# Hybrid decoder layer on one core: score products that alternate between row halves, low-rank products stacked over 128 rows, one product for a chunk's right-hand side, dt projected in 16 columns

## The chip, the cores and the metric

The kernel runs on one core of one Trainium2 chip. A core has five engines with queues of their own, each in order: TensorE (PE in the profile; its weight loads are PEld), VectorE (DVE), ScalarE (ACT), GpSimd (POOL), and SyncE (SP), which here issues the DMA transfers. Matmuls write to PSUM, everything else lies in SBUF or in DRAM. The metric is the device time of one execution in microseconds; the time before is 2901.62 us, the median of three runs (2898.83 to 2908.35).

## What is computed

One layer of a hybrid decoder for a prompt of 2048 tokens and, with the same weights, eight sampled tokens. One input projection feeds two head groups, RWKV-7 time mixing and a Mamba-2 scan; their outputs go through one output projection, a LayerNorm, a squared-ReLU MLP and a second LayerNorm. Cut to the parts that the change touches:

```python
proj = x @ w_in                                   # 1024 -> 3336 columns
u = pr + (prev - pr) * mu_shift                   # token shift
r, k, v, uw, ua, ug = split(u)                    # uw and ua: 64 columns each
w_log = -softplus(-(w0 + tanh(uw) @ w_up)) - 0.5  # w_up, a_up: 64 x 512
a = sigmoid(a0 + ua @ a_up)
# per token and head (8 heads of 64), state S is 64 x 64:
Sa = S @ (-kk)
S = S * decay + Sa * (kk * a) + v * k
y = S @ r
dt = softplus(dt + dt_bias)                       # 8 columns of proj
```

The other parts of the layer are the same before and after.

## The kernel before, in words

The prompt goes in four blocks of 512 tokens. First `project` runs over the four blocks: 27 tiles of output columns, each 8 contraction tiles long. The fp32 operands are split into a high and a low fp32r part (`split`, lines 189 and 190: one ACT copy and one subtraction on DVE or POOL), and a product is three one-pass matmuls (`mm3`, lines 156 to 158). The tile of dt has 8 columns; it is projected in the same way, so its 24 matmuls a block have 8 output columns and 512 moving ones. `evict` takes each tile from PSUM. For every pair of heads `pair` makes decay and `a`: two fp32 products with 64 contraction rows, `waup[0:64]` with the upper half of the tile `uwa` and `waup[64:128]` with the lower half (lines 526 and 527). An fp32 product leaves two records in the profile. `pair` writes its results to DRAM (`s_ar`, `s_bk`, `s_v` and others), chunk by chunk.

The mixers then work on chunks of 64 tokens, eight a block, 32 in all. `rwkv` loads a chunk (`ar`, `bk`, `uv`) and makes the score products, line 591: eight fp32 products, four pairs of heads by two row halves, with 64 contraction rows each. Half j writes the PSUM tile `pss[j]`. Both are of tag "m", which has two buffers, shared with the other mixers. Masked, the scores go to `sc`; a triangular inverse follows (`masked`, tiles xs), and ends in `xf`. `chain` carries the state `S` (tag "st") through the chunks: the right-hand side `pr` is the sum of two products per head, scores times v and `ar` times S (lines 675 and 677); `rr`, `pu`, the new `uv`, the outputs `py` and the new state follow. `mamba` and `rwkv_post` are the other mixers.

`tail` is the output projection and the MLP of a block. The mixers of the next block are woven into the bulk matmuls of `project` and `tail` by `drive`, which gives each a step for so many microseconds of bulk. The order within an engine's queue is then set by a list scheduler when the program is built: it places whatever its estimate says is ready. Two products that stand side by side in the source can thus stand apart in PE's queue.

Of the kernel before, what the change touches and what calls it, by code (L numbers as in the profile page):

```python
# [18 lines left out]
FIRST = 4  # L19
POOLA, POOLO, POOLF = 4, 2, 0  # L20
# [87 lines left out]
class K:  # L108
# [41 lines left out]
    def mm(self, out, l, r, start=True, stop=True):  # L150
        self.nc.tensor.matmul(out, l, r, start=start, stop=stop)  # L151
# [71 lines left out]
    def setup_mix(self):  # L223
# [51 lines left out]
        self.waup = c("waup", (128, 512))  # L275
        nc.sync.dma_start(self.waup, A["waup"])
# [49 lines left out]
    def wpieces(self, j, halves=(0, 1)):  # L326
        out = []
        w = TILES[j][1]
        for h in halves:
            if w == 128:  # L330
                src = self.A["w_in"][j if j < T_DT else j - 1, :, h * 512:(h + 1) * 512]
            else:
                src = self.A["w_dt"][:, h * 32:(h + 1) * 32]
            out.append(self.wpiece(src, (4, w)))
        return out

    def project(self, b, ahead):
# [13 lines left out]
        for j in range(NT):  # L351
            w = TILES[j][1]
            if b == 0 and j < len(self.first):
                pieces = self.first[j]
            else:
                pieces = self.wpieces(j)
            if j == NT - 2:
                nxt = ahead()
            banks = []
            for o, n, _ in segs:  # L360
                ps = self.ps("b")
                for k in range(KT):
                    l = [pieces[k // 4][i][:, k % 4, :] for i in range(2)]
                    r = [act[k][:, i, o:o + n] for i in range(2)]
                    self.mm3(ps[:w, :n], l, r, k == 0, k == KT - 1)
# [14 lines left out]
    def evict(self, b, j, mains):  # L380
        nc, st = self.nc, self.blkst[b]
        if j < T_DT:
# [22 lines left out]
            if j == T_UWA:  # L405
                nc.scalar.activation(u[0:64], u[0:64], AF.Tanh)
            elif j == T_UG:
# [11 lines left out]
        else:  # L419
            i = j - T_Z  # L420
            th = self.pair_tile()[0][:, :TB]
            for o, m, ps in mains:
# [4 lines left out]
                              th.rearrange("p (u t) -> p u t", u=4))  # L427

# [36 lines left out]
    def delta(self, b, mains):  # L465
        nc, st = self.nc, self.blkst[b]
        raw = self.pair_tile()[0]
        for o, m, ps in mains:
            nc.scalar.activation(raw[0:8, o:o + m], ps, AF.Copy)
        pt = self.ps("a", (128, 4, 8))  # L470
        for u in range(4):
            self.tr(pt[:, u, :], raw[0:8, u * 128:(u + 1) * 128])
        dt = self.sm("dt", [128, 4, 8], bufs=4)
        nc.vector.tensor_tensor(out=dt, in0=pt, in1=self.dtb.unsqueeze(1).to_broadcast([128, 4, 8]), op=ALU.add)
# [28 lines left out]
    def pair(self, b, hp):  # L503
# [22 lines left out]
        self.mm(pw, self.waup[0:64, cs], uwa[0:64])  # L526
        self.mm(pa, self.waup[64:128, cs], uwa[64:128])
# [15 lines left out]
        for u in range(4):  # L543
# [22 lines left out]
        nc.sync.dma_start(self.s_bk[b][:, 64:128, hp, :].rearrange("c p x -> p c x"),  # L566
                          BK[64:128].rearrange("p c a t -> p c (a t)"))
        for a in range(2):
            nc.sync.dma_start(self.s_bk[b][:, 0:64, hp, (1 - a) * 64:(1 - a) * 64 + 64].rearrange("c p x -> p c x"),
                              BK[0:64, :, a, :])  # L570
# [3 lines left out]
    def rwkv(self, b, c):  # L574
# [8 lines left out]
        for j in range(2):  # L583
            nc.sync.dma_start(uv[H[j], j], self.s_v[b][c // 2, 64 * (c % 2):64 * (c % 2) + 64, :, 64 * j:64 * j + 64])
# [4 lines left out]
        for hp in range(4):  # L589
            for j in range(2):  # L590
                self.mm(pss[j][:, hp, :], bk[H[j], hp, :], ar[H[j], hp].rearrange("p a t -> p (a t)"))
        for j in range(2):
            nc.vector.tensor_tensor(out=sc[:, j], in0=pss[j],
                                    in1=self.con("scm").unsqueeze(1).to_broadcast([128, 4, 128]), op=ALU.mult)
            for g in range(4):
                p0 = 64 * (1 - j) + 16 * g
                nc.sync.dma_start(d_l[1 - j, g].rearrange("h s t -> s h t"), sc[p0:p0 + 16, j, :, 16 * g:16 * g + 16])
# [31 lines left out]
        def masked(x, m):  # L629
            p = pt()  # L630
            for hp, e in idx:
                self.mm(p[H[e], hp, :], sc[H[e], 1 - e, hp, 0:64], x[H[e], hp, :])
# [21 lines left out]
        g2 = masked(x2, "m2")  # L654
        yield
# [8 lines left out]
    def chain(self, b, c):  # L664
# [20 lines left out]
        nc.scalar.activation(uv[H[1], 0], pu[H[1]], AF.Copy)  # L685
        nc.vector.tensor_copy(uv[H[0], 1], pu[H[0]])
# [201 lines left out]
    def sample(self):  # L888
# [35 lines left out]
        for hp in range(4):  # L924
            self.mm(pw[:, hp, :], self.waup[0:64, hp * 128:(hp + 1) * 128], us[0:64, 0, :])
# [7 lines left out]
        for hp in range(4):  # L933
            self.mm(pa[:, hp, :], self.waup[64:128, hp * 128:(hp + 1) * 128], us[64:128, 0, :])
# [137 lines left out]
        nc.vector.tensor_scalar(out=dd[0:8, 0, :], in0=P[0:8, T_DT, :], scalar1=hb[0:8, 0:1], scalar2=None, op0=AD)  # L1072
# [505 lines left out]
```

## Time and profile before

| what | before |
|---|---|
| median of 3 runs | 2901.62 us |
| the profiled execution | 2905.99 us, of which the span is 2904.2 us |
| mean granted TensorE clock | 0.985 |
| first and last 400 us: PE busy | 388.54 of the first 400.00, 400.05 of the last 424.00 |
| DMA | 395.34 MB, mean 136 GB/s |

The span goes from the first to the last instruction. A row of the grouped view has the line, the engine, the operation, the tile written and those read, the shape (contraction rows * output columns, then output rows x moving columns), the count, the busy time in us and the mean of one in ns, and the engine's idle time before them. A row of the timeline has the start in us, the duration in us, and the same names; rows that follow on each other are merged, with their count.

### The profile page before, as it was taken

To read this page: it belongs to the slowest core of one execution; us is meant where nothing else is said; L and a number is where in the kernel's file an instruction comes from. 1 tells how busy PE (TensorE), PEld (TensorE's weight loads), DVE (VectorE), ACT (ScalarE), POOL (GpSimd) and SP (SyncE) were. 2 spreads that over 40 slices of the span, in tenths; PEclk is the share of its full clock that TensorE was granted. 3 is DMA by queue.
4 is the path that set the end of the run, shared out by engine and by line. 5 is a ranking of instruction groups with operands and counts; after the bars stand their busy time and mean duration, and the time that the engine had idled before them with its cause. 6 is when DMAs were issued, how large, how long until landed. Compare 5 with 4: busy or idle time off the path is not lost.

```text
span 2904.2 us, 53242 instructions
## 1 busy us (share of the span) xinstructions
PE 2825.7 (97%) x19648; PEld 2331.7 (80%) x19648; DVE 1963.2 (68%) x4765; ACT 1249.2 (43%) x2391; POOL 356.6 (12%) x510
## 2 busy tenths in 40 slices
PE   9999999999999999999999999998999999899997
PEld 6798987777788777788888888887877878888886
DVE  6767868867857777686866666568766655754446
ACT  4454544543536333344544344335443334543332
POOL 2221212211221000001300000022000000300001
PEclk9999999999999999999999999999999999999999
DMA  6654654554645444355523344254343334433232
GB/s 191 182 174 122 176 179 139 165 175 136 178 144 162 129 124 119 114 160 176 175 89 106 116 122 120 76 174 165 114 137 110 108 106 162 164 99 94 91 100 71
DMA packets 334169, 395.34 MB, mean 136 GB/s; under 512 B 85518, under 2 KB 191588, under 8 KB 333900
## 3 DMA queue, kind: packets, MB, share of 16 engines
q1 hardware_dynamic: 333908, 391.94, 44.8%
q8 instruction: 154, 2.52, 0.4%
q14 instruction: 107, 0.88, 0.1%
HBM read 331.06 MB, written 60.81 MB: 135 GB/s over the span
## 4 chain that ended last, share of the span: by engine, by line
PE 83%; DVE 9%; DMA 4%; issue 2%; ACT 2%; SPq 0%; POOL 0%; DVEq 0%; ACTq 0%; POOLq 0%
PE psb L156 19%; PE psb L157 18%; PE psb L158 18%; PE psm L151 7%; PE psa L156 4%; PE psa L157 4%; PE psa L158 4%; PE psc L151 2%; PE psa L151 2%; PE psm L163 1%; PE psy L694 1%; PE psb L151 1%; DVE w L190 1%; DMA wr<-in_w_in_dram 1%; DVE g L1176 1%
## 5 line engine op out<-in xcount | busy, mean ns | idle before, releaser
L189 ACT ACTIVATE w<-wr 128x512 fp32r<-128x512 f32 (+1 forms) x840 | 521.0, 625 | 693.2 <-PE psb L158 272.3
L190 DVE TENSOR_TENSOR w<-wr,w 128x512 fp32r<-128x512 f32 x714 | 511.0, 722 | 255.7 <-ACT w L189 247.0
L156 PE MATMUL psb<-act,w 128*128 128x512 f32 (+3 forms) x1796 | 637.4, 356 | 5.7 <-ACT act L189 5.0
L157 PE MATMUL psb<-act,w 128*128 128x512 f32 (+3 forms) x1796 | 630.0, 351 | 0.0
L158 PE MATMUL psb<-act,w 128*128 128x512 f32 (+3 forms) x1796 | 628.3, 350 | 0.0
L156 PEld LDWEIGHTS psb<-act,w 128*128 128x128 f32 (+1 forms) x1796 | 337.9, 189 | 61.5 <-ACT act L189 6.3
L158 PEld LDWEIGHTS psb<-act,w 128*128 128x128 f32 (+1 forms) x1796 | 338.4, 189 | 51.4 <-issue 3.3
L157 PEld LDWEIGHTS psb<-act,w 128*128 128x128 f32 (+1 forms) x1796 | 339.1, 189 | 46.1 <-DVE act L190 1.3
L156 PE MATMUL psb<-w,g 128*128 128x512 f32 x788 | 315.7, 403 | 0.2 <-ACT w L189 0.2
L157 PE MATMUL psb<-w,g 128*128 128x512 f32 x788 | 312.4, 396 | 0.0
L158 PE MATMUL psb<-w,g 128*128 128x512 f32 x788 | 311.4, 395 | 0.0
L190 POOL TENSOR_TENSOR w<-wr,w 128x512 fp32r<-128x512 f32 (+1 forms) x126 | 181.5, 1445 | 564.6 <-ACT w L189 546.4
L1453 DVE TENSOR_TENSOR g<-psb,g 128x512 f32<-128x512 f32 x173 | 118.9, 688 | 158.2 <-PE psb L158 157.8
L156 PEld LDWEIGHTS psb<-w,g 128*128 128x128 f32 x788 | 148.0, 188 | 36.5 <-ACT w L189 0.6
L158 PEld LDWEIGHTS psb<-w,g 128*128 128x128 f32 x788 | 148.0, 188 | 34.5 <-issue 0.3
L157 PEld LDWEIGHTS psb<-w,g 128*128 128x128 f32 x788 | 148.4, 188 | 32.5 <-issue 0.2
L190 DVE TENSOR_TENSOR g<-r,g 128x256 fp32r<-128x256 f32 (+1 forms) x172 | 97.2, 565 | 87.4 <-ACT g L189 86.3
L1403 ACT ACTIVATE r<-psb 128x512 f32<-128x512 f32 (+2 forms) x130 | 63.3, 488 | 208.9 <-PE psb L158 205.7
L156 PE MATMUL psa<-act,w 128*128 128x256 f32 (+2 forms) x336 | 115.7, 344 | 0.0
L157 PE MATMUL psa<-act,w 128*128 128x256 f32 (+2 forms) x336 | 114.1, 340 | 0.0
L158 PE MATMUL psa<-act,w 128*128 128x256 f32 (+2 forms) x336 | 113.5, 338 | 0.0
L156 PE MATMUL psb<-g,w 128*128 128x264 f32 (+3 forms) x324 | 108.9, 336 | 1.2 <-DVE g L400 0.8
(376 smaller groups left out, 5237.2 us busy)
## 6 DMA issues: line engine op xcount, KB each, us to landing
wr<-in_w_ff_dram SPq DMA_DIRECT2D x512, 256.0 KB
wr<-in_w_in_dram SPq DMA_DIRECT2D x208, 256.0 KB
wr<-in_w_out_dram SPq DMA_DIRECT2D x112, 256.0 KB
lr<-d_l SPq DMA_DIRECT2D x256, 64.0 KB
s_m<-g SPq DMA_DIRECT2D x48, 256.0 KB
ms<-s_m SPq DMA_DIRECT2D x16, 768.0 KB
wr<-in_xT_dram SPq DMA_DIRECT2D x32, 256.0 KB
s_ar<-g SPq DMA_DIRECT2D x16, 512.0 KB
```

The costliest lines, as they stand in the source:

```text
L151: self.nc.tensor.matmul(out, l, r, start=start, stop=stop)
L156: nc.tensor.matmul(out, l[0], r[0], start=first, stop=False)
L157: nc.tensor.matmul(out, l[0], r[1], start=False, stop=False)
L158: nc.tensor.matmul(out, l[1], r[0], start=False, stop=last)
L163: self.nc.tensor.transpose(out, in_, self.cst[p0:p0 + k, o + p0:o + p0 + k])
L189: nc.scalar.activation(hi, raw, AF.Copy)
L190: (eng or nc.vector).tensor_tensor(out=lo, in0=raw, in1=hi.bitcast(F32), op=ALU.subtract)
L694: acc = lambda o, l, r, start, stop: nc.tensor.matmul(o, l, r, start=start, stop=stop, skip_group_check=True)
L1176: eng.tensor_tensor(out=h, in0=h, in1=b[:p], op=ALU.add)
L1403: nc.scalar.activation(rl, ps, AF.Relu)
L1453: self.nc.vector.tensor_tensor(out=h, in0=ps, in1=h, op=ALU.add)
```

## The change

Four parts and what goes with them.

- Scores. `row` ties the eight score products together: each is queued right behind the one before it, with a high priority, in the order of the source, where the halves j = 0 and 1 alternate. A memset of one element of `pss[1]` on DVE stands ahead of the first, so the row is queued only when both PSUM tiles are to be had.
- Low-rank products. `w_up` and `a_up` are each laid over both halves of the 128 rows and split into high and low parts (`wup`). `stacked` lays the high part of the operand over one half of the rows and its low part over the other. A product is then two fp32r matmuls with 128 contraction rows in place of one fp32 product with 64. The sample takes the same parts, in fp32 and 64 rows, with two products in place of one.
- Right-hand side. In `sc` the 64 rows that held no scores for a half now take `ar`, by two ACT copies a chunk; in `uv` the rows that are later filled by `pu` first take S, by one copy on ACT and one on DVE. One product with 128 rows replaces two with 64. For this the halves of `bk`, `uv` and `sc` change places; the DMAs keep their sizes and number.
- dt. High and low parts of its weights are put side by side as 16 columns. Two matmuls per contraction tile replace three; the two halves are added on DVE. The weights come in one DMA and one split rather than two.

`dynamic_dma_scratch_size=256` sets aside less SBUF for transfers that POOL issues; the kernel has none.

```diff
+    def row(self, args, held):
+        prev = self.mm(*args[0])
+        self.tc.add_manual_dep(prev.ins, held.ins.name, mybir.DependencyInfo(
+            mybir.DependencyClass.NoSync, mybir.DependencyReason.DATA), reason="bank")
+        for a in args[1:]:
+            with self.tc.high_priority(RANK), self.tc.issue_after(prev.ins):
+                prev = self.mm(*a)
...
-        self.waup = c("waup", (128, 512))
-        nc.sync.dma_start(self.waup, A["waup"])
+        self.wup = []
+        for i in range(2):
+            raw = self.sb("wr", (128, 512))
+            for h in range(2):
+                nc.sync.dma_start(raw[64 * h:64 * h + 64], A["waup"][64 * i:64 * i + 64])
+            self.wup.append([self.mp.tile([128, 512], F32R, name=f"wup{i}{s}") for s in range(2)])
+            self.split(raw, *self.wup[i])
...
+                    if j == T_DT:
+                        l = pieces[:, k].rearrange("p s c -> p (s c)")
+                        self.mm(ps[:w, :n], l, r[0], k == 0, False)
+                        self.mm(ps[:w, :n], l, r[1], False, k == KT - 1)
+                    else:
+                        l = [pieces[k // 4][i][:, k % 4, :] for i in range(2)]
+                        self.mm3(ps[:w, :n], l, r, k == 0, k == KT - 1)
...
+    def stacked(self, u):
+        nc = self.nc
+        hl = self.sb("g4", (128, 2, 520), F32R)
+        W, a = hl[:, 0, :TB], hl[:, 1, :TB]
+        lo, hi = slice(0, 64), slice(64, 128)
+        for t, x, y in ((W, lo, hi), (a, hi, lo)):
+            nc.scalar.activation(t[x], u[x], AF.Copy)
+            nc.vector.tensor_tensor(out=t[y], in0=u[x], in1=t[x].bitcast(F32), op=ALU.subtract)
+        return W, a
...
-        self.mm(pw, self.waup[0:64, cs], uwa[0:64])
-        self.mm(pa, self.waup[64:128, cs], uwa[64:128])
+        for p, w, x in ((pw, self.wup[0], uwa[0]), (pa, self.wup[1], uwa[1])):
+            self.mm(p, w[0][:, cs], x, True, False)
+            self.mm(p, w[1][:, cs], x, False, True)
...
-        for hp in range(4):
-            for j in range(2):
-                self.mm(pss[j][:, hp, :], bk[H[j], hp, :], ar[H[j], hp].rearrange("p a t -> p (a t)"))
+        held = nc.vector.memset(pss[1][0:1, 0, 0:1], 0.0)
+        self.row([(pss[j][:, hp, :], bk[H[j], hp, :], ar[H[j], hp].rearrange("p a t -> p (a t)"))
+                  for hp in range(4) for j in range(2)], held)
...
         g2 = masked(x2, "m2")
+        for j in range(2):
+            nc.scalar.activation(sc[H[j], j, :, 0:64], ar[H[j], :, 0, :], AF.Copy)
...
+        nc.scalar.activation(uv[H[0], 0], S[H[0]], AF.Copy)
+        nc.vector.tensor_copy(uv[H[1], 1], S[H[1]])
         for hp in range(4):
             for j in range(2):
-                self.mm(pr[H[1 - j], hp, :], sc[H[j], j, hp, 0:64], uv[H[j], j, hp, :], True, False)
-            for j in range(2):
-                self.mm(pr[H[1 - j], hp, :], ar[H[j], hp, 0, :], S[H[j], hp, :], False, True)
+                self.mm(pr[H[j], hp, :], sc[:, j, hp, 0:64], uv[:, j, hp, :])
```

Three places of PE's queue show what the scheduler makes of it. The first is the score row of the fourth chunk of the first block, while the second block is projected (psm are the two score tiles, psb is the bulk tile that is being summed). Before, the four products of one half and the four of the other stand eight bulk matmuls apart:

```order
L151 MATMUL psm_4557<-ar_4537,bk_4539 128x128 x4
L158 MATMUL psb_4616<-g_248_1643,w_4588 128x256
L156 MATMUL psb_4616<-g_250_1650,w_4588 128x256
L157 MATMUL psb_4616<-g_250_1650,w_4588 128x256
L158 MATMUL psb_4616<-g_250_1650,w_4588 128x256
L156 MATMUL psb_4616<-g_252_1657,w_4588 128x256
L157 MATMUL psb_4616<-g_252_1657,w_4588 128x256
L158 MATMUL psb_4616<-g_252_1657,w_4588 128x256
L156 MATMUL psb_4616<-act_1732,w_4593 128x256
L151 MATMUL psm_4558<-ar_4537,bk_4539 128x128 x4
```

In the changed kernel the same row stands in one place, and the tiles of the two halves take turns:

```order
L166 MATMUL psb_4645<-act_1766,w_4597 128x264
L152 MATMUL psm_4560<-ar_4471,bk_4473 128x128
L152 MATMUL psm_4561<-ar_4471,bk_4473 128x128
L152 MATMUL psm_4560<-ar_4471,bk_4473 128x128
L152 MATMUL psm_4561<-ar_4471,bk_4473 128x128
```

Two more such pairs follow, and then the bulk tile goes on. Of the 32 rows, 7 alternated before; now all do.

The second place is a pair of heads in the first block, the products for decay (psa) and a (psb). Before, there is one fp32 product each, in two places among the bulk:

```order
L151 MATMUL psb_718<-g_32_310,waup 128x512
L156 MATMUL psb_746<-act_184,w_738 128x512
L157 MATMUL psb_746<-act_184,w_738 128x512
L163 MATMUL psa_708<-cst,arsy_84_652 8x128
L158 MATMUL psb_746<-act_184,w_738 128x512
L156 MATMUL psb_746<-act_189,w_738 128x512
L157 MATMUL psb_746<-act_189,w_738 128x512
L151 MATMUL psa_717<-g_32_310,waup 128x512
```

Now there are two fp32r matmuls in each place, of the shape of the bulk:

```order
L152 MATMUL psb_737<-g_35_328,wup_271 128x512
L152 MATMUL psb_737<-g_35_328,wup_272 128x512
L166 MATMUL psb_767<-act_184,w_759 128x512
L167 MATMUL psb_767<-act_184,w_759 128x512
L168 MATMUL psb_767<-act_184,w_759 128x512
L166 MATMUL psb_767<-act_189,w_759 128x512
L173 MATMUL psa_727<-cst,arsy_87_671 8x128
L167 MATMUL psb_767<-act_189,w_759 128x512
L168 MATMUL psb_767<-act_189,w_759 128x512
L166 MATMUL psb_767<-act_194,w_759 128x512
L152 MATMUL psa_736<-g_35_328,wup_264 128x512
L152 MATMUL psa_736<-g_35_328,wup_265 128x512
```

The third place is a right-hand side (psc) of the first block, which stands behind products of the triangular inverse (psm from xs). Before:

```order
L151 MATMUL psm_5317<-xs_5155,xs_5236 64x64 x8
L151 MATMUL psc_5328<-uv_4541,sc_4555 64x64 x2
L151 MATMUL psc_5328<-st_4925,ar_4537 64x64 x2
L151 MATMUL psc_5328<-uv_4541,sc_4555 64x64 x2
L151 MATMUL psc_5328<-st_4925,ar_4537 64x64 x2
```

The last four rows come once more, and transposes follow. Now eight products stand there:

```order
L173 MATMUL psa_5313<-cst,g_735_5120 128x128 x4
L152 MATMUL psm_5325<-xs_5158,xs_5241 64x64 x8
L152 MATMUL psc_5336<-uv_4475,sc_4558 64x64 x8
L173 MATMUL psm_5353<-cst,ms_5349 128x128 x4
L173 MATMUL psm_5365<-cst,ms_5349 128x128 x2
```

The products with S are gone; those that are left have 128 contraction rows, which differs from the 64 of the products ahead of them. Over the program, PE's right-hand sides stood in 13 groups of their own before, and otherwise in one group with products of 64 rows; they now stand in 41 groups of their own.

More of the change, by code (lines that the diff above doesn't have):

```diff
@@ L19 @@
 FIRST = 4
+RANK = 4000
 POOLA, POOLO, POOLF = 4, 2, 0
@@ L150, in mm @@
     def mm(self, out, l, r, start=True, stop=True):
-        self.nc.tensor.matmul(out, l, r, start=start, stop=stop)
+        return self.nc.tensor.matmul(out, l, r, start=start, stop=stop)
+    def row(self, args, held):
[5 more added lines that the diff above has]
+                prev = self.mm(*a)
     def mm3(self, out, l, r, first, last):
@@ L329, in wpieces, with wdt @@
         for h in halves:
[L330 to L333, printed above, removed]
+            src = self.A["w_in"][j if j < T_DT else j - 1, :, h * 512:(h + 1) * 512]
             out.append(self.wpiece(src, (4, w)))
         return out
+    def wdt(self):
+        raw = self.sb("wr", (128, 512))[:, :64]
+        self.nc.sync.dma_start(raw, self.A["w_dt"])
+        t = self.sb("w", (128, 2, 512), F32R)[:, 0, :128].rearrange("p (k s c) -> p s k c", k=KT, s=2)
+        self.split(raw.rearrange("p (k c) -> p k c", k=KT), t[:, 0], t[:, 1])
+        return t.rearrange("p s k c -> p k s c")
     def project(self, b, ahead):
@@ L351, in project @@
         for j in range(NT):
-            w = TILES[j][1]
-            if b == 0 and j < len(self.first):
+            w = 128 if j != T_DT else 16
+            if j == T_DT:
+                pieces = self.wdt()
+            elif b == 0 and j < len(self.first):
                 pieces = self.first[j]
@@ L362, in project @@
                 for k in range(KT):
-                    l = [pieces[k // 4][i][:, k % 4, :] for i in range(2)]
                     r = [act[k][:, i, o:o + n] for i in range(2)]
-                    self.mm3(ps[:w, :n], l, r, k == 0, k == KT - 1)
+                    if j == T_DT:
+                        l = pieces[:, k].rearrange("p s c -> p (s c)")
[4 more added lines that the diff above has]
+                        self.mm3(ps[:w, :n], l, r, k == 0, k == KT - 1)
                 banks.append(ps)
@@ L468, in delta @@
         for o, m, ps in mains:
-            nc.scalar.activation(raw[0:8, o:o + m], ps, AF.Copy)
-        pt = self.ps("a", (128, 4, 8))
+            nc.scalar.activation(raw[0:16, o:o + m], ps, AF.Copy)
+        pt = self.ps("a", (128, 4, 16))
         for u in range(4):
-            self.tr(pt[:, u, :], raw[0:8, u * 128:(u + 1) * 128])
+            self.tr(pt[:, u, :], raw[0:16, u * 128:(u + 1) * 128])
         dt = self.sm("dt", [128, 4, 8], bufs=4)
-        nc.vector.tensor_tensor(out=dt, in0=pt, in1=self.dtb.unsqueeze(1).to_broadcast([128, 4, 8]), op=ALU.add)
+        nc.vector.tensor_tensor(out=dt, in0=pt[:, :, 0:8], in1=self.dtb.unsqueeze(1).to_broadcast([128, 4, 8]), op=ALU.add)
+        nc.vector.tensor_tensor(out=dt, in0=pt[:, :, 8:16], in1=dt, op=ALU.add)
         self.softplus(dt.rearrange("p a b -> p (a b)"), 32)
@@ L924, in sample @@
         for hp in range(4):
-            self.mm(pw[:, hp, :], self.waup[0:64, hp * 128:(hp + 1) * 128], us[0:64, 0, :])
+            for i in range(2):
+                self.mm(pw[:, hp, :], self.wup[0][i][0:64, hp * 128:(hp + 1) * 128].bitcast(F32), us[0:64, 0, :], i == 0, i == 1)
         w = V6[:, 1]
@@ L933, in sample @@
         for hp in range(4):
-            self.mm(pa[:, hp, :], self.waup[64:128, hp * 128:(hp + 1) * 128], us[64:128, 0, :])
+            for i in range(2):
+                self.mm(pa[:, hp, :], self.wup[1][i][64:128, hp * 128:(hp + 1) * 128].bitcast(F32), us[64:128, 0, :], i == 0, i == 1)
         a = t(4, 8)
@@ L1071, in sample @@
         dd = t(2, 8)
-        nc.vector.tensor_scalar(out=dd[0:8, 0, :], in0=P[0:8, T_DT, :], scalar1=hb[0:8, 0:1], scalar2=None, op0=AD)
+        pd = self.ps("m", (128, 8))
+        self.mm(pd[0:8], self.con("s16", 0, 16), P[0:16, T_DT, :])
+        nc.vector.tensor_scalar(out=dd[0:8, 0, :], in0=pd[0:8], scalar1=hb[0:8, 0:1], scalar2=None, op0=AD)
         self.softplus(dd[0:8, 0, :], 8, 8)
```

23 lines of the change are left out of this document (12 added, 11 removed).

## The prediction

> **What bounds the kernel now.** I read the page first: the busy row, then the chain that ended last.
>
> ```profile
> span 2904.2 us, 53242 instructions
> PE 2825.7 (97%) x19648; PEld 2331.7 (80%) x19648; DVE 1963.2 (68%) x4765; ACT 1249.2 (43%) x2391; POOL 356.6 (12%) x510
> PE 83%; DVE 9%; DMA 4%; issue 2%; ACT 2%; SPq 0%; POOL 0%; DVEq 0%; ACTq 0%; POOLq 0%
> ```
>
> TensorE (PE) is busy for 97% of the span and carries 83% of the chain; 2904.2 - 2825.7 = 78.5 us is all that it is not busy. The longest causes in the waits view of PE (columns: who waited, for what; sum in us, times, longest) are these.
>
> ```profile
> PE psb L163 <- DVE g L1257: 7.9, 3, 4.7
> PE psm L151 <- DVE sc L593: 6.0, 5, 4.5
> PE psb L156 <- ACT act L189: 5.0, 1, 5.0
> ```
>
> None is a wait that returns every chunk. So time taken off PE's queue comes off the end, unless PE then meets new waits. "Busy" is not the price of a matmul, though: consecutive ones overlap. The price is the distance between two starts, which the timeline gives. Three prices follow, for work that the change removes.
>
> ```profile
> 1003.43 1.16 PE L151 MATMUL psm<-ar,bk 64*128 64x128 f32 x16 [0.66 <-DMA bk<-s_bk]
> 1004.52 0.50 PE L156 MATMUL psb<-act,w 128*128 128x512 f32 x1
> ...
> 907.95 1.74 PE L151 MATMUL psm<-ar,bk 64*128 64x128 f32 x16
> 909.62 0.39 PE L156 MATMUL psb<-act,w 128*128 128x256 f32 x1
> ...
> 387.69 0.28 PE L157 MATMUL psb<-g,w 128*128 128x256 f32 x1
> 387.90 1.16 PE L151 MATMUL psm<-ar,bk 64*128 64x128 f32 x8
> 388.98 0.38 PE L158 MATMUL psb<-g,w 128*128 128x256 f32 x1
> 389.21 0.28 PE L156 MATMUL psb<-g,w 128*128 128x256 f32 x1
> 389.33 0.28 PE L157 MATMUL psb<-g,w 128*128 128x256 f32 x1
> ...
> 390.37 1.16 PE L151 MATMUL psm<-ar,bk 64*128 64x128 f32 x8 [0.17 <-DVE sc L593]
> 391.45 0.38 PE L157 MATMUL psb<-act,w 128*128 128x256 f32 x1
> ```
>
> These are the score products of three chunks (an fp32 product leaves two records, so eight products are 16). In the chunk at 1003 the row halves alternate: 1004.52 - 1003.43 = 1.09 us. At 907 three of one half come in a row, three of the other, then one and one: 1.67 us. At 387 and 390 each half has its four in a place of its own: 1.08 us twice. Two halves that alternate run side by side; four of one half do not. And a visit of narrow products costs something around itself: the step of a 256-column matmul is 0.12 us (389.21 to 389.33), but 0.21 just before the visit and 0.23 just after it, so 0.20 us outside the visit's own time.
>
> **Scores.** Followed through the whole trace, 7 chunks alternate, 14 take 1.67 us, 9 are split into two visits, and two are irregular (about 2.1 and 1.4 us without idle time). In the changed order all 32 alternate. 14 x 0.58 = 8.1; 9 x (2.16 + 0.20 - 1.09) = 11.4; the two others 1.3: 20.8 us. The grouped row says the same by another way:
>
> ```profile
> L151 PE MATMUL psm<-ar,bk 64*128 64x128 f32 x512 | 58.0, 287 | 5.9 <-DVE xs L634 2.5 <-DMA bk<-s_bk 2.0 <-DVE sc L593 1.3
> L151 PE MATMUL psb<-g,waup 64*128 64x512 f32 x32 | 18.0, 641 | 0.0
> L151 PE MATMUL psa<-g,waup 64*128 64x512 f32 x32 | 18.0, 641 | 0.0
> L151 PE MATMUL psm<-ms,waup 64*128 64x8 f32 x16 | 2.1, 255 | 0.0
> L157 PE MATMUL psb<-act,w 128*8 128x512 f32 x20 | 7.9, 396 | 0.0
> L685 ACT ACTIVATE uv<-psc 64x256 f32<-64x256 f32 x32 | 12.1, 379 | 41.7 <-PE psc L151 41.3
> L686 DVE COPY uv<-psc 64x256 f32<-64x256 f32 x32 | 13.1, 410 | 1.2 <-ACT uv L685 1.2
> ```
>
> 58.0 us busy against 32 x 1.16 = 37.1 is 20.9. I take **21 us**, from 19 to 23.
>
> **Low-rank products.** The two waup rows are 32 products of 512 columns, two records each.
>
> ```profile
> 64.34 1.12 PE L151 MATMUL psb<-g,waup 64*128 64x512 f32 x2
> 65.39 0.50 PE L156 MATMUL psb<-act,w 128*128 128x512 f32 x1
> 65.73 0.40 PE L157 MATMUL psb<-act,w 128*128 128x512 f32 x1
> ...
> 66.55 0.39 PE L157 MATMUL psb<-act,w 128*128 128x512 f32 x1
> 66.86 1.12 PE L151 MATMUL psa<-g,waup 64*128 64x512 f32 x2
> ...
> 68.25 0.39 PE L156 MATMUL psb<-act,w 128*128 128x512 f32 x1
> 68.48 0.40 PE L157 MATMUL psb<-act,w 128*128 128x512 f32 x1
> ```
>
> A product alone holds PE for 65.39 - 64.34 = 1.05 us; 24 do so, and four pairs that stand together take 1.50 us a pair: 31.2 us. After it there are 64 one-pass (fp32r) products of 128 rows and 512 columns, of the shape of the bulk, whose step is 68.48 - 68.25 = 0.23 us: 14.9. The 28 visits also go: 0.08 before (66.55 to 66.86 is 0.31) and 0.11 after (0.34) is 5.3 us, of which I leave out a quarter for those that stand beside other narrow products. 31.2 - 14.9 + 4 = **20 us**, from 16 (visits worth nothing) to 22. The operand must be split once a block: two ACT copies and two DVE subtractions of 64x512, eight each in all, well under 1 us apiece; ACT at 43% and DVE at 68% hide them. Uncovered, they would cost about 2 us a block. The start gains 256 KB of loads and two splits; PE waits for nothing there after its first 5.0 us, so I take 0, at most 2.
>
> **dt.** 24 products a block become 16, each still of 512 columns and so 0.23 us (8 output columns take the 396 ns of the row above, as the bulk's 128 do): 8 x 4 x 0.234 = **7.5 us**.
>
> **Right-hand side.** Sixteen products a chunk become eight.
>
> ```profile
> 592.39 0.40 PE L158 MATMUL psb<-act,w 128*128 128x512 f32 x1
> 592.72 0.51 PE L151 MATMUL psm<-xs,xs 64*64 64x64 f32 x10
> ...
> 593.29 0.28 PE L151 MATMUL psc<-uv,sc 64*64 64x64 f32 x4
> 593.41 0.28 PE L151 MATMUL psc<-st,ar 64*64 64x64 f32 x4
> ...
> 593.88 0.28 PE L151 MATMUL psc<-st,ar 64*64 64x64 f32 x4
> 594.09 0.77 PE L163 MATMUL psm<-cst,ms 128*128 128x128 f32 x5
> ```
>
> Four records take 0.12 us (593.29 to 593.41), the last four 0.21 with the way out. Sixteen records fewer are 0.47 us a chunk, 15 us in all. But here the products share their visit with xs products of the same 64x64 shape, as in some 23 of the 32 chunks. The new ones are 128x64, a shape of their own, in 41 groups where before 13 stood alone: 28 visits more, at 0.20 us outside and some 0.05 for the entry, is 7 us back. I take **8 us**, from 0 to 15.
>
> [...]
>
> **Sample and the rest.** The sample's eight waup products (2.1 us) become sixteen: 2 us more. Per chunk ACT gets three copies of 64x256 and DVE one, 0.38 and 0.41 us by rows L685 and L686, and DVE a memset of one element: 36 us of ACT and about 15 of DVE over 2300 us, under other work. What is not hidden is their place. The copies of ar into sc wait on ACT for the last masked product, and splits of weights queue behind them; the copies of S into uv lie between the state update and the right-hand side that PE takes next in order. Bulk stands between in most chunks. I put 0.1 us a chunk on this, **3 us more**, from 5 less (places of the present waits shift) to 18 more (half a microsecond a chunk).
>
> **The sum.** 21 + 20 + 7.5 + 8 - 2 - 3 = 51.5 us off the profiled execution's own 2905.99 us (the span and 1.8 us around it): 2854.5. That execution is 4.4 us above the median of the runs shown, 2901.62, so 2850.
>
> **Rivals.** *Waits take half.* PE is fed by splits on ACT and DVE; work that leaves PE leaves them less time. For it: DVE at 68% is in places the next engine. Against: no repeated PE wait for a split in the list above. Half of 54.5 us (the sum without its last term): 2874. *The shapes cost nothing.* If the new groups mostly lie beside other narrow ones, the right-hand side gives its 15 us, and with a few waits less the time is 2835. *PE is not what sets the end*, and the work leaves as idle time: 2900; 97% busy speaks against it. *Slower.* A row of scores now begins only when both psm banks are free, by the memset in DVE's queue, and PE takes its queue in order: a row that is late holds all the bulk behind it. It decides at 54.5 / 32 = 1.7 us a chunk; at 3 us a chunk the time is 2901.6 - 54.5 + 96 = 2943. The longest wait of PE for DVE's score product is 4.5 us, but all five together are 6.0, and the changed order puts the rows into running bulk groups. *The change doesn't do what it says* is ruled out by the order: all rows alternate, and the shapes are there.
>
> **How the numbers follow.** Forecast (2840 to 2865) 0.58; cheaper shapes 0.17; half lost 0.15; no effect 0.05; slower 0.05. Within 0.3% is about what a measurement here can tell from no change: faster 0.90, same 0.05, slower 0.05. The ends: all terms at their best with 5 us fewer waits are 23 + 22 + 7.5 + 15 - 2 + 5 = 70.5, so 2831; all at their worst with 18 us of waits are 19 + 16 + 7.5 + 0 - 2 - 18 = 22.5, so 2879. What lies outside is under 2 in 10.
>
> **What would show it.** psm<-ar,bk falls from 58.0 us busy to about 37, with all 32 visits at 1.09 us. The waup rows give way to 64 records of 128x512 near 400 ns; dt rows read 128*16, 48 rather than 72 at full width. psc<-st,ar is gone, and psc<-uv,sc is 128*64 at about 24 us. PE's busy time falls by about 50 us while what it is not busy stays near 78. Wrong would be PE waits on uv, sc or the memset that repeat every chunk, or score rows that alternate and still take more than 1.2 us.

## The result, and the profile after

The changed kernel takes 2881.95 us (median of four runs, 2878.82 to 2886.13); beside it the kernel before took 2904.98 us (four runs, 2898.83 to 2909.46). The ratio is 0.9923, with a 95% interval of 0.9906 to 0.994: faster, by 23 us. The forecast was 2850, its range 2831 to 2879; the time lies 3 us above the range, as much as the median of the kernel before moved between its first three runs (2901.62) and these four.

The page of the changed kernel, with the busy row and the shares of the chain:

```profile
span 2880.1 us, 52319 instructions
...
PE 2786.3 (97%) x19114; PEld 2310.9 (80%) x19114; DVE 1979.4 (69%) x4841; ACT 1285.9 (45%) x2493; POOL 364.5 (13%) x508
...
PE 79%; DVE 10%; DMA 4%; issue 4%; ACT 2%; SPq 1%; POOL 0%; DVEq 0%; POOLq 0%; ACTq 0%
```

PE is busy 39.4 us less (2825.7 before), but what it is not busy rose from 78.5 to 2880.1 - 2786.3 = 93.8 us. PE's waits (who waited, for what; sum, times, longest):

```profile
PE psb L166 <- ACT w L199: 13.9, 5, 9.3
PE psb L173 <- DVE g L1308: 9.9, 4, 4.7
PE psb L166 <- ACT act L199: 5.5, 2, 5.2
...
PE psb L167 <- DVE w L200: 4.4, 1, 4.4
...
PE psm L152 <- issue: 2.7, 3, 1.3
```

Before, the rows that answer to the first and the fourth are these.

```profile
PE psb L156 <- ACT w L189: 2.7, 2, 2.5
PE psb L157 <- DVE w L190: 2.3, 1, 2.3
```

New are one wait of 9.3 us for a split of weights, in the first row, and the one of 4.4. All of PE's waits for splits on ACT, DVE and POOL (those over 0.15 us, without the first of the program) make 8.4 us before and 22.7 after. The groups that answer to those of before (busy, mean ns | idle ahead):

```profile
L152 PE MATMUL psm<-ar,bk 64*128 64x128 f32 x512 | 39.3, 294 | 8.7 <-DVE xs L677 4.1 <-issue 2.7 <-DVE psm L632 1.7
L152 PE MATMUL psc<-uv,sc 128*64 128x64 f32 x512 | 26.5, 233 | 1.6 <-ACT sc L700 1.4
L152 PE MATMUL psb<-g,wup 128*128 128x512 f32 x32 | 14.5, 535 | 0.0
L152 PE MATMUL psa<-g,wup 128*128 128x512 f32 x32 | 10.8, 420 | 0.0
L152 PE MATMUL psb<-act,w 128*16 128x512 f32 x40 | 9.8, 395 | 0.0
L152 PE MATMUL psm<-ms,wup 64*128 64x8 f32 x32 | 3.9, 254 | 0.0
```

Scores fell from 58.0 to 39.3 us, the waup rows gave way to 64 records of 128x512, dt has 16 columns, and psc<-st,ar is gone. The change does what it says.

To set all this against the forecast's terms I go through PE's records and give each the time from its start to the start of the next one, less the idle time ahead of that one, and less half of the time at half clock, that is, in which the trace has a granted clock of 0.50. "Work" is the sum of these; idle and half clock stand apart. The half is an estimate: in the changed kernel ten steps between the starts of the bulk's 128x512 matmuls take 2.33 us at full clock (1167.25 to 1169.58) and five take 2.14 at half (1177.13 to 1179.27), by which 0.46 of that time would be lost. From the two traces, in us:

| part | before | after | forecast | measured |
|---|---|---|---|---|
| scores | 55.2 | 35.1 | -21 | -20.1 |
| low-rank, with its neighbours and the sample's | 53.5 | 38.7 | -20 + 2 | -14.8 |
| dt | 22.7 | 15.1 | -7.5 | -7.6 |
| right-hand side, and the xs products beside it | 108.7 | 103.4 | -8 | -5.3 |
| bulk | 2261.5 | 2262.4 | 0 | +0.9 |
| the rest | 292.4 | 294.0 | 0 | +1.6 |
| **work** | 2794.0 | 2748.7 | **-54.5** | **-45.3** |
| idle between records | 58.8 | 73.8 | +3 with the next | +15.0 |
| lost to half clock | 31.4 | 37.2 | | +5.8 |

The work that left is 9 us short of the forecast. The waits were put at 3 us and are 21. So the question of the experiments: do these 21 us belong to one part?

### The profile page after: what moved, and what is told of

It reads as the page before. It is cut to its first block, busy times and chain, and to the rows that moved or that the text cites. A ratio compares the mean times of both kernels' runs of the same rounds, so it can differ in the third digit from the quotient of the medians.

```text
span 2880.1 us, 52319 instructions
## 1 busy us (share of the span) xinstructions
PE 2786.3 (97%) x19114; PEld 2310.9 (80%) x19114; DVE 1979.4 (69%) x4841; ACT 1285.9 (45%) x2493; POOL 364.5 (13%) x508
## 4 chain that ended last, share of the span: by engine, by line
PE 79%; DVE 10%; DMA 4%; issue 4%; ACT 2%; SPq 1%; POOL 0%; DVEq 0%; POOLq 0%; ACTq 0%
PE psb L166 18%; PE psb L167 18%; PE psb L168 17%; PE psm L152 7%; PE psa L166 4%; PE psa L168 4%; PE psa L167 4%; PE psc L152 2%; PE psa L152 2%; PE psb L152 1%; DVE w L200 1%; PE psm L173 1%; PE psy L741 1%; DVE lr L655 1%; DVE rX L656 1%
## 5 line engine op out<-in xcount | busy, mean ns | idle before, releaser
L166 PE MATMUL psb<-act,w 128*128 128x512 f32 (+2 forms) x1768 | 628.4, 356 | 6.3 <-ACT act L199 5.5
L167 PE MATMUL psb<-act,w 128*128 128x512 f32 (+2 forms) x1768 | 621.1, 352 | 0.6 <-DVE act L200 0.6
L168 PE MATMUL psb<-act,w 128*128 128x512 f32 (+2 forms) x1768 | 616.9, 349 | 0.0
L166 PEld LDWEIGHTS psb<-act,w 128*128 128x128 f32 x1768 | 335.9, 190 | 55.5 <-ACT act L199 6.0
L168 PEld LDWEIGHTS psb<-act,w 128*128 128x128 f32 x1768 | 336.3, 190 | 45.6 <-DVE w L200 0.2
L167 PEld LDWEIGHTS psb<-act,w 128*128 128x128 f32 x1768 | 337.0, 191 | 44.7 <-DVE act L200 2.6
L200 POOL TENSOR_TENSOR w<-wr,w 128x512 fp32r<-128x512 f32 x124 | 180.2, 1458 | 717.5 <-ACT w L199 703.6
L166 PEld LDWEIGHTS psb<-w,g 128*128 128x128 f32 x788 | 148.6, 189 | 46.1 <-ACT w L199 10.3
L655 DVE TENSOR_TENSOR lr<-rX,lr 128x4 f32<-128x4 f32 (+14 forms) x480 | 100.7, 210 | 10.8
```

The lines of the kernel that those rows point to most:

```text
L166: nc.tensor.matmul(out, l[0], r[0], start=first, stop=False)
L167: nc.tensor.matmul(out, l[0], r[1], start=False, stop=False)
L168: nc.tensor.matmul(out, l[1], r[0], start=False, stop=last)
L200: (eng or nc.vector).tensor_tensor(out=lo, in0=raw, in1=hi.bitcast(F32), op=ALU.subtract)
L655: nc.vector.tensor_tensor(out=row, in0=X[:, :, s + 1:16], in1=row, op=ALU.mult)
```

## The experiments

Each kernel is timed beside the kernel before, whose medians there lie between 2902.26 and 2904.98 us. Work, idle and half clock are those of its profiled execution; the clock is the mean over all its runs. For only low-rank the profiled execution, 2906.77 us, is 8 us above the median, so its half clock is not typical.

| kernel | median us | ratio, 95% interval | work | idle | half clock | mean clock |
|---|---|---|---|---|---|---|
| before | 2904.98 | | 2794.0 | 58.8 | 31.4 | 0.986 |
| **changed** | 2881.95 | 0.9906 to 0.9940 | 2748.7 | 73.8 | 37.2 | 0.982 |
| only scores | 2918.16 | 1.0030 to 1.0066 | 2777.5 | 80.4 | 36.8 | 0.982 |
| only low-rank | 2898.37 | 0.9966 to 0.9996 | 2778.6 | 62.1 | 43.8 | 0.984 |
| only dt | 2906.99 | 0.9990 to 1.0021 | 2786.2 | 58.7 | 36.6 | 0.984 |
| only right-hand side | 2903.08 | 0.9986 to 1.0012 | 2788.2 | 60.1 | 33.2 | 0.986 |
| only scores, no memset | 2911.51 | 1.0019 to 1.0047 | 2791.6 | 68.3 | 29.9 | 0.984 |
| changed, no memset | 2888.31 | 0.9938 to 0.9972 | 2758.0 | 69.1 | 38.9 | 0.982 |
| changed, weights first | 2885.10 | 0.9924 to 0.9955 | 2751.8 | 74.0 | 39.0 | 0.983 |
| changed less scores | 2891.95 | 0.9951 to 0.9974 | 2769.0 | 65.4 | 30.9 | 0.983 |
| changed less low-rank | 2890.92 | 0.9934 to 0.9968 | 2764.5 | 70.0 | 30.5 | 0.984 |
| changed less right-hand side | 2882.96 | 0.9902 to 0.9947 | 2755.1 | 70.8 | 38.6 | 0.983 |
| changed, rate 0.32 | 2888.76 | 0.9924 to 0.9959 | 2749.4 | 78.4 | 39.1 | 0.981 |
| changed, rate 0.40 | 2890.25 | 0.9936 to 0.9963 | 2749.1 | 72.2 | 44.8 | 0.980 |
| changed, rate 0.45 | 2892.32 | 0.9947 to 0.9973 | 2749.4 | 76.3 | 44.2 | 0.980 |
| changed, rate 0.55 | 2895.50 | 0.9959 to 0.9982 | 2749.9 | 78.5 | 44.6 | 0.981 |
| before, rate 0.45 | 2909.89 | 1.0015 to 1.0033 | 2796.3 | 62.5 | 31.9 | 0.985 |
| changed, later rate 0.20 | 2937.82 | 1.0093 to 1.0133 | 2746.8 | 118.4 | 45.9 | 0.971 |
| changed, second block untied | 2886.83 | 0.9926 to 0.9958 | 2751.4 | 64.7 | 48.4 | 0.981 |
| the same, rate 0.38 | 2889.33 | 0.9933 to 0.9968 | 2749.3 | 68.7 | 45.0 | 0.981 |

Among the kernels made from the changed one, those less scores and at rates 0.45, 0.55 and the later 0.20 have intervals that lie wholly above its own; for the others the intervals touch, and a difference of 1 to 9 us in their medians is an indication.

### Each part alone

The kernel before, with the lines of one part of the diff and no others. The first theory was that the waits come only with all parts together.

> The kernel before with the score rows alone changed (row and its memset). All three theories expect about 20 us less PE work in psm<-ar,bk (58 us busy to about 39). Theory A (work leaves as predicted; about 21 us came back only where all four parts together let the bulk run ahead of the mixers and the sample): PE idle within 5 us of before, time 15 to 20 us shorter. Rival B (the memset and the rows tied together hold the bulk up each chunk): time at most 10 us shorter, PE idle up by 8 us or more, with waits of psm on the memset. Rival C (the scheduler's static order decides where stalls fall, by chance): idle moves by more than 5 us in either direction at a few places, none of them at a score row.

> The kernel before with the low-rank products alone changed. Work removed as read from the two traces: about 15 us (not 20, since the visits around the products did not get cheaper), all of it while the input projection runs. Theory A: 12 to 15 us shorter, PE idle within 5 us of before. Rival B (splits of the operand and loads at the start cost time): under 8 us shorter, with PE waits on g or wup. Rival C: idle moves by more than 5 us at a few places away from the changed products.

> The kernel before with dt in 16 columns alone. Work removed: 7.6 us. Theory A: 6 to 8 us shorter. Rival B has no mechanism here and expects the same. Rival C: anything from 15 us shorter to 5 us longer, with idle time or half-clock time that moves by more than 5 us away from dt.

> The kernel before with the right-hand side alone as one product, with its copies of ar and S. Work removed by the traces: 11.5 us in the products, 6 us back in the xs products beside them, so 5 to 6 net. Theory A: 3 to 6 us shorter, idle within 5 us of before. Rival B (the copies lie in each chunk's chain and PE waits for them): no shorter or up to 10 us longer, with PE waits on sc or uv of 0.1 us a chunk or more. Rival C: idle moves by more than 5 us at places that have nothing to do with the copies. For the four single parts together: A expects a sum of 38 to 48 us, more than the 23 us of the whole change; B a sum near 23 us; C any sum.

Work fell by 16.5, 15.4, 7.8 and 5.8 us, 45.5 in all, against 45.3 for the whole: it adds up. The times don't: against the median beside them (2904.52) they are +13.6, -6.2, +2.5 and -1.4 us, 8.5 us *slower* in all (by the four intervals together some 0 to 18; dt and the right-hand side alone can't be told from no change), where the whole is 23 faster. The first theory fell. The scores alone gained 21.6 us of idle time. The group of score products, and the longest of their waits in the timeline (start, duration):

```profile
L152 PE MATMUL psm<-ar,bk 64*128 64x128 f32 x512 | 41.1, 299 | 20.3 <-issue 13.0 <-DVE xs L645 5.9 <-DVE g L1268 0.9
```

```profile
1132.87 0.06 DVE L600 MEMSET psm<- 1x1 f32 x1
...
1141.34 0.40 PE L166 MATMUL psa<-act,w 128*128 128x512 f32 x1
...
1147.24 0.69 DVE L749 TENSOR_TENSOR q<-q,q 128x512 f32<-128x512 f32 x1 [10.30 <-DMA q<-s_bv]
1147.85 0.69 DVE L200 TENSOR_TENSOR w<-wr,w 128x512 fp32r<-128x512 f32 x1
1148.46 0.68 DVE L756 TENSOR_TENSOR q<-psm,q 128x512 f32<-128x512 f32 x1
...
1149.24 2.08 PE L152 MATMUL psm<-ar,bk 64*128 64x128 f32 x16 [7.51 <-issue]
```

DVE waited 10.3 us for a transfer of another mixer, whose psm tile it reads only at 1148.46. The row starts 0.1 us after that read ends, so I take that tile for one of the two that the row needs; the row stood next in PE's queue, and the bulk behind it waited 7.5 us. The memset did not hold the row here: it ran at 1132.87, 16 us earlier, so the tile that it writes was had by then and the row stood for the other one. This is the forecast's rival "slower" (a late row holds the bulk behind it), with a price of 20.3 - 5.9 = 14.4 us in this order.

### The memset, the ring of weights, and the whole without the scores

No memset: the line `held = ...` and the dependency on it go, and the products stay tied. Weights first: four weight loads go ahead of the next block's inputs.

```diff
             if last:
+                for dh in range(1 if b == 0 else 0):
+                    w2s.append([self.wpiece(A["w_ff2"][f * 128:(f + 1) * 128, dh * 512:dh * 512 + 512], (1, 512))
+                                for f in range(4 * g, 4 * g + 4)])
                 nxt = before_last(b)
```

> The score rows alone, without the memset that holds a row back until both psm tiles are free (the products are still tied to each other). With the memset PE stood idle 20.3 us ahead of psm<-ar,bk (5.9 before). Theory D (a row that is queued in one piece waits for the second PSUM tile, which another mixer holds while DVE waits for a DMA; that wait holds all bulk behind it): if the memset is what puts the rows there, idle ahead of psm<-ar,bk falls under 9 us and the time to 2890 to 2902. If the tie itself does it, idle there stays over 14 us and the time within 5 us of 2918. Rival C (the stall at 1149 us is an accident of this order): idle ahead of the score rows falls, but as much comes back at other places, time 2908 to 2918.

> The changed kernel without that memset. In the changed kernel PE stood idle 8.7 us ahead of psm<-ar,bk. Theory D: the memset cost little in this order, so the time is 2875 to 2886 and idle there 4 to 9 us. Rival B (the memset is what slows the whole change): 10 us or more shorter, under 2872. Rival C: anything, 2865 to 2900, with idle time that moves at places away from the rows.

> The changed kernel, with the first four weight pieces of the last MLP group of the first block asked for before the output tiles of the next block (which wait for the sample and hold the ring wr). PE stood idle there for 9.3 us at 1313, with 17.1 us at half clock around it. Theory D (that stall is the ring's, and costs its 9.3 us and up to 8 us of half clock): the gap goes, time 2865 to 2873. Rival F (bulk has simply caught up with the sample's chain, and PE stands a little later for the same chain, at w_out or act of the next block): the gap moves behind 1313, time 2877 to 2886.

> The changed kernel with the score products in their old order (the other three parts kept). If the parts' times simply add, taking away a part that alone cost 14 us makes it faster: 2868 or less. If the scores' 20 us of PE work show once the other parts are there (theory D: work leaves, and stalls depend on what meets what): 2892 to 2903. Between these: the rows' waits take part of the 20 us.

Without the memset the group of the scores alone reads:

```profile
L152 PE MATMUL psm<-ar,bk 64*128 64x128 f32 x512 | 51.3, 295 | 11.1 <-DVE xs L642 6.6 <-DVE q L753 2.2 <-ACT m L984 1.4
```

Idle ahead of the rows fell by 9.2 us, but busy rose by 10.2: the rows no longer alternate throughout. So with the scores alone the memset costs 7 us, though it takes 14 us of work off, and in the whole it is worth 6, by medians whose intervals overlap. Without scores the whole is 10 us slower, so the part that alone cost 14 us is worth 10 in company. Weights first missed theory D and came out as rival F had it, at 2885 us: the wait of 9.3 us was gone, and one of 4.1 stood 2 us later.

That wait is the largest new one. In the changed kernel (ACT, DVE, SP, then PE):

```profile
1299.03 4.81 ACT L199 ACTIVATE act<-wr 128x512 fp32r<-128x512 f32 x7 [12.64 <-PE psb L168]
...
1302.08 0.75 DVE L1159 TENSOR_SCALAR m<-m,ms 128x1024 f32<-128x1024 f32 x1 [2.42 <-DMA m<-in_state_ssm_dram]
...
1306.99 4.29 DVE L200 TENSOR_TENSOR act<-wr,act 128x512 fp32r<-128x512 f32 x7
...
1308.88 0.90 SPq L206 DMA_DIRECT2D wr<-in_w_ff_dram  x2
...
1303.47 0.40 PE L168 MATMUL psb<-act,w 128*128 128x512 f32 x1
1313.19 1.22 PE L166 MATMUL psb<-w,g 128*128 128x512 f32 x2 [9.32 <-ACT w L199]
```

All seven buffers of `wr` hold inputs of the next block. ACT has copied them by 1304, but DVE, in order, is in the sample's state loop and subtracts only from 1306.99 on; until then SP cannot load the weights that PE needs. Before, the sample ended while bulk was still running (PE, DVE, PE):

```profile
1318.69 0.38 PE L163 MATMUL psm<-cst,m 8*128 8x8 f32 x4 [0.41 <-DMA m<-d_y]
...
1337.46 4.87 DVE L190 TENSOR_TENSOR act<-wr,act 128x512 fp32r<-128x512 f32 x7 [0.67 <-ACT act L189]
...
1342.51 0.99 PE L156 MATMUL psb<-w,g 128*128 128x512 f32 x3 [0.24 <-ACT w L189]
```

There 23.8 us lay between the sample's last transposes and the first product of the block's last weights, and PE waited 0.24 us. In the changed kernel PE is ready for that product at 1303.9, 39 us earlier than it started before; the sample's last transposes come at 1314.77, 4 us earlier. With the wait the granted clock went to half: 0.50 from 1306.10 to 1323.16. Windows of 17 us of the changed kernel (start:end, length, busy us of PE, PEld, DVE, ACT, POOL, then PEclk):

```profile
1289.00:1306.00 17.00, 14.87 (x64) 11.67 (x63) 13.33 (x17) 6.29 (x10) 0.00 (x0) 1.00 0.47 117
1306.00:1323.00 17.00, 9.81 (x34) 7.50 (x35) 11.71 (x27) 5.47 (x10) 0.00 (x0) 0.50 0.57 192
1323.00:1340.00 17.00, 16.96 (x111) 14.70 (x109) 9.28 (x20) 7.65 (x15) 5.21 (x4) 1.00 0.53 176
```

### The pace of the sample's chain

The next theory was that tied rows stretch the chain of the second block's mixers, behind which the sample stands. The order shows it: between the first and the last score row of that block 190 us of bulk matmuls stood in PE's queue before, and 221 stand there now, counted in the built order (in the traces 1060 and 1188 bulk matmuls). The rate at which the steps are woven in changes that and no work:

```diff
-RATE_M0, RATE_M, RATE_S = 0.2, 0.23, 0.35
+RATE_M0, RATE_M, RATE_S = 0.2, 0.23, 0.4
```

> The changed kernel with the step rate of the second block's mixers and the sample raised from 0.35 to 0.40 steps per us of bulk. In the built order, counted in us of bulk matmuls ahead, the eight score rows of the second block's mixers take 190 us before and 221 in the changed kernel (216 with the score rows alone changed, 190 to 195 with any of the other parts alone), and the sample's last transposes come 130 us of bulk ahead of the next block's MLP before, 110 after; at 0.40 it is 205 and 123. Theory G (tied score rows stretch the chain of the mixers and the sample, so that the bulk, now shorter, arrives at the end of the first tail before the sample is done): the idle time of PE between 1300 and 1320 (9.9 us) falls to under 5, time 2872 to 2879. Rival C (accidents of the order): that idle goes, but comes back elsewhere, time 2878 to 2890.

> The same at 0.45: the chain takes 192 us of bulk, the sample ends 142 ahead. Theory G: no stall at the end of the first tail, time 2868 to 2876. Rival C: 2878 to 2890. If a denser chain meets its own limits (transfers and DVE), waits at the score rows of the second block grow and the time is no better than at 0.40.

> The same at 0.55: the chain takes 180 us of bulk, the sample ends 150 ahead. Theory G: no more than at 0.45, 2866 to 2878, since the sample has then time to spare and the chain runs into its own transfers.

> The kernel before at 0.45, as a control: 167 us of bulk for the chain, the sample ends 167 ahead of the next MLP. Before, PE had only 0.7 us idle at the end of the first tail, so theory G expects no gain: 2900 to 2908. If the rate itself were worth something, 2895 or less.

The stall shrank as expected (idle between 1200 and 1400 us: 9.9 us in the changed kernel, then 7.6, 6.7 and 5.2), and the time got worse each time, by 8, 10 and 14 us. At the beginning of the same tail, between 800 and 1000 us, idle rose from 13.8 to 16.8, 20.7 and 24.8 us, and the half clock took 7 us more. The control lost 7 us as well. The gain was given back a few hundred us earlier.

### One part out of the whole, and other orders

> The changed kernel with the right-hand side in two products, as before (the other three parts kept). Theory H (each part takes its PE work off in every kernel; on top of it the time moves by some 8 us with the order, by idle time and half clock that no part owns): 5.6 us of work come back, so 2880 to 2895, with other work in PE's classes within 3 us of the changed kernel. Rival R (the copies and the new shapes of this part cause the idle time of the whole change): under 2879, with PE idle at least 8 us below the 73.8 us of the changed kernel.

> The changed kernel with the low-rank products as before. Theory H: 14.8 us of work come back, 2888 to 2904. Rival R2 (the parts stand in each other's way, so that the last one added is worth nothing): 2878 to 2886.

> The changed kernel with the step rate of the second block's mixers and the sample at 0.32 rather than 0.35; no product, copy or transfer is added or removed. Denser (0.40) cost 8 us. Theory H: the PE work is the same within 3 us, the time anywhere from 2874 to 2890, by idle and half clock alone. Theory G2 (the density of the mixers' steps in the first tail sets the stalls, and the lowest rate that still ends in time is best): 2870 to 2876, with less idle between 750 and 950 us and no more than before at 1313.

> The changed kernel with the step rate of the third and fourth block's mixers at 0.20 rather than 0.23, so that only the second and third tail are ordered otherwise. Theory H: PE work the same within 3 us, 2874 to 2890. Theory G2: 2870 to 2877, with less idle in the second and third tail (25.7 us there in the changed kernel).

No part owns the idle time: without the right-hand side it is 3 us lower, without the low-rank products 4, without scores 8. Low-rank is worth 9 us in company, the right-hand side 1. A rate of 0.32 costs 7 us with the work unchanged. The later rate of 0.20 missed every expectation, with the same work and 56 us more time. Of the 44.6 us of idle that it adds, 20 are the waits of the first row here; the second row is a score row that stood 9.3 us for a psm tile which DVE had still to read. PE's waits and the wait itself:

```profile
PE psb L166 <- ACT w L199: 34.1, 5, 21.2
PE psm L152 <- DVE q L792: 9.3, 1, 9.3
```

```profile
2470.57 0.80 PE L166 MATMUL psb<-w,g 128*128 128x512 f32 x1 [21.25 <-ACT w L199]
```

It is the wait of 1313 us again, at the end of the third tail. In SP's queue the block's last weights stand behind the inputs of the next block, and those behind the mixers that write them (SP's timeline of this kernel):

```profile
2460.11 4.72 SPq L322 DMA_DIRECT2D wr<-s_o  x8
2465.26 3.67 SPq L206 DMA_DIRECT2D wr<-in_w_ff_dram  x4
```

Mixers that are not through when the bulk comes to its last group hold it up.

### The second block untied

```diff
+        args = [(pss[j][:, hp, :], bk[H[j], hp, :], ar[H[j], hp].rearrange("p a t -> p (a t)"))
+                for hp in range(4) for j in range(2)]
+        if b == 1:
+            for x in args:
+                self.mm(*x)
+        else:
+            self.row(args, nc.vector.memset(pss[1][0:1, 0, 0:1], 0.0))
```

> The changed kernel, with the score rows of the second block alone (those in the first tail, ahead of the sample) in the old way: not tied and without the memset. By the built order their chain takes 195 us of bulk in place of 221 and the sample ends 130 us of bulk ahead of the next block's MLP in place of 110. About 4 us of score work come back there (8.7 to 12.8). Theory G (the tied rows stretch that chain, and the stall at the end of the first tail is its price: 9.3 us idle and about 5 us of half clock): idle from 1280 to 1350 us falls from 9.9 to under 6, PE's classes else unchanged, time 2870 to 2879. Theory H (any order has such stalls somewhere): 2880 to 2892, with the idle time back at other places.

> The same with the step rate there at 0.38 in place of 0.35: the chain takes 190 us of bulk and the sample ends 142 ahead. Theory G: the rest of that stall goes too, 2867 to 2877. Theory H, and what the rates 0.40 to 0.55 have shown: the stall shrinks, but denser steps cost as much at the beginning of the tail, 2880 to 2892.

Half of it held. In the first of the two the wait for the ring is gone, idle fell by 9.1 us to 64.7, and one wait is left there, for the sample's own transfer:

```profile
1293.87 0.41 PE L173 MATMUL psm<-cst,m 8*128 8x8 f32 x4 [3.81 <-DMA m<-d_y]
```

But the half clock rose by 11.2 us in that execution (over all its runs the mean clock is 0.981 against 0.982), 2.7 us of work came back, and the time is 5 us worse. At rate 0.38 that wait is there still, 4.9 us at 1280 us, and the time is 2889 us, in theory H's range. So in the changed kernel that stall comes with the tied rows (with the scores alone, the same rows leave only 3.5 us idle there), and its removal did not shorten the kernel.

No kernel tried here beats the changed one.

## Why the prediction was wrong, step by step

- **PE sets the end, so work that leaves comes off.** Right for the work: 45.3 us left, and it adds up part by part. Wrong in that a part's time follows from it: alone, the four parts together gained nothing.
- **Scores, 21 us.** Measured 20.1. In the chunk at 978.78 us the visit takes 1.09 us, as forecast:

```profile
978.78 1.16 PE L152 MATMUL psm<-ar,bk 64*128 64x128 f32 x16
979.87 0.69 PE L152 MATMUL psc<-uv,sc 128*64 128x64 f32 x16
```

- **dt, 7.5 us.** Measured 7.6.
- **Low-rank, 20 us, less 2 for the sample.** Measured 14.8: the sample took 1.8, and the other 16.6 are what the products were sized at (31.2 - 14.9 = 16.3). The 4 us for the bulk around the visits can't be seen in the whole, where bulk is 0.9 us up. They can't be ruled out either: in the two pairs of kernels that differ by this part alone, bulk is 3.3 and 2.8 us lower with it, while among the kernels with the low-rank change it lies anywhere from 2258 to 2266 us.
- **Right-hand side, 8 us.** Measured 5.3: 11.6 off the products, 6.3 back in the xs products, which now stand alone. The new visits cost about what was forecast (7); the products gave less than 15, and that is the part of the term that was mis-sized. Of the 0.25 us a visit that the forecast uses, 0.20 is read from the trace around the visits at 387 and 390 us, and the 0.05 for the entry was the author's estimate, which no row shows; the 6.3 us that were seen are 0.23 for each of the 28 visits that it counted.
- **New waits, 3 us more, at most 18.** This is the step that failed: idle 15.0 and half clock 5.8, together 20.8. Of the 27 us by which the profiled execution fell short of the forecast's 51.5, 18 are here and 9 are work. The term was priced as 0.1 us a chunk for the copies into sc and uv. Such waits are there and small: 1.4 us for sc L700 in the group of psc<-uv,sc. What came instead is not repeated each chunk. PE's waits for splits went from 8.4 to 22.7 us, nearly all of the 15.0, and two single ones are 13.7 of these 22.7: 9.3 us where the bulk caught up with the sample, and 4.4 at 844 us, where a split stands on DVE behind small operations of the mixers:

```profile
842.90 0.98 DVE L655 TENSOR_TENSOR lr<-rX,lr 128x20 f32<-128x20 f32 x1
843.81 0.68 DVE L200 TENSOR_TENSOR w<-wr,w 128x512 fp32r<-128x512 f32 x1
844.54 0.58 PE L167 MATMUL psb<-w,act 128*128 128x256 f32 x1 [4.45 <-DVE w L200]
```

The forecast let the waits of before shift only to its gain ("from 5 less"); the runs at unchanged work show that they move with a new order, here mostly to its loss. It also had no term for the clock.

- **Rivals.** "Waits take half" (2874, at 0.15) came nearest, and what was added to PE's idle time is waits for splits, as it said; but they are long ones at two places, not a feed that runs short everywhere, and a third of the miss is work that did not leave. "Slower", by a held row, was ruled small since the rows stand in running bulk; with the scores alone it took 14.4 us, in the whole 8.7 - 5.9 = 2.8. "No effect" and "the shapes cost nothing" are out: the work fell, and 6.3 us came back in xs.

What stays open: why the half clock takes 30 us in one order and 48 in another with as much idle time. The traces show it mostly where PE stood idle, as below, but don't foretell it. Nor does a run show why the whole does better than its parts alone, beyond that the order is another.

## What to carry to other kernels

The work that left the busy engine was sized here from distances between starts to within 0.1 to 3.2 us a part. In this statically ordered queue the stalls were drawn anew with each order, and that moved the time by up to 14 us at unchanged work, and once by 56; so the forecast of a change needs that much room, on the side of loss where the kernel before has few stalls. Look first for the places where a side chain must end before the bulk goes on (here the sample and the ring `wr`): a shorter bulk comes there earlier (39 us here), the chain hardly (4 us).

## What was not expected of the hardware

**Half clock came in steps of 3.413 us.** In the traces of the kernel before and of the changed one the stretches at a granted clock of 0.50 begin on one grid of 3.413 us and last one to five steps of it, but for the last one, which runs past the program's end. In that of the later rate 0.20 the clock is 0.50 from 2440 to 2473 us, over nine steps. Each of the twenty traces of this study is cut into windows on its own grid. These are the windows at full clock between PE's first and last matmul, and how many were followed by one at half clock:

| share of the window in which PE was idle | windows | next at half clock |
|---|---|---|
| under 40% | 15984 | 46 |
| 40 to 50% | 97 | 29 |
| 50 to 60% | 75 | 63 |
| over 60% | 121 | 121 |

A window at half clock with over 20% idle was followed by another in 153 of 154 cases. Two waits of PE of nearly the same length, in the changed kernel:

```profile
795.79 0.28 PE L173 MATMUL psa<-cst,hist 128*24 128x128 f32 x1 [2.08 <-DVE g L1469]
...
816.82 0.68 PE L152 MATMUL psm<-xs,sc 64*64 64x64 f32 x16 [2.11 <-DVE xs L660]
```

After the first the clock stays at full up to 817.99 us; after the second it is 0.50 from 817.99 to 824.82. 29 runs of the kernel before have clocks of 0.982 to 0.989, and take 2.3 us less for each 0.001 more.

**Half clock stood after the sample's narrow products.** With the low-rank change the sample has 32 records of 8 columns in place of 16. In the kernel with the second block untied, PE's timeline and its windows there (PEclk is the sixth value after the length, the counts left out):

```profile
1147.73 1.95 PE L152 MATMUL psm<-ms,wup 64*128 64x8 f32 x16
1149.61 0.51 PE L167 MATMUL psb<-w,g 128*128 128x512 f32 x1
...
1150.27 3.01 PE L152 MATMUL psm<-ms,wup 64*128 64x8 f32 x16
```

```profile
1147.50:1150.90 3.40, 3.40 (x27) 2.89 (x25) 0.71 (x2) 0.23 (x1) 0.00 (x0) 1.00 0.22 63
1150.90:1157.70 6.80, 6.80 (x24) 5.91 (x25) 2.29 (x14) 0.46 (x2) 0.00 (x0) 0.50 0.07 20
```

PE was busy for all of the first window, and still the granted clock was 0.50 for the next 6.8 us, which counts above as 3.4 lost. In the changed kernel the two groups of such records stand at 1171.34 and 1173.88 us, and the clock is 0.50 from 1176.39 to 1179.80; in the kernel before the 16 stand from 1176.7 to 1180.3, and the clock stays at full. Of the 13 kernels with 32 such records 12 have a stretch of 3.4 to 10.2 us at half clock right there, without idle time; of the 7 with 16, one has. That the narrow products bring it is not shown beyond this count: a sample that keeps one product for the two was not tried.
